# The low part of every second v block, subtracted by GpSimd instead of VectorE

## The chip, the cores and the metric

The kernel runs on one core of a Trainium2 chip. The metric is the device time of one execution in microseconds; lower is better. The median of three runs of the kernel before is 2388.8 us (2382.14 to 2390.61).

## The reference

One inference step of a two-layer encoder trunk for two groups of requests: 256 prompt rows and 8 x 16 sample rows, each row 1024 wide. Layer 0 mixes rows by a short gated convolution, layer 1 by stick-breaking attention; after each comes PEER, a mixture of 16384 single-row experts per layer, of which every row chooses 8 x 16 by product keys:

```python
def block(xb):
    q = (xb @ w_q).reshape(PEER_BLOCK, PEER_HEADS, 2, PEER_HALF).astype(jnp.float32)
    s = jnp.einsum("thpc,hpnc->thpn", q, subkeys.astype(jnp.float32))
    s_top, i_top = lax.top_k(s, K)
    ...
    g = jax.nn.softmax(best, axis=-1)
    act = jax.nn.gelu(jnp.einsum("td,thkd->thk", xb, u_tab[expert]), approximate=False)
    wgt = (g * act.astype(jnp.float32)).astype(xb.dtype)
    return jnp.einsum("thk,thkd->td", wgt, v_tab[expert])
```

Each mixer and each PEER is followed by x <- LayerNorm(ALPHA * x + sublayer(x)).

## The kernel before, in words

The two groups take different ways. The **sample rows** gather their experts: `peer_gather` fetches, for each of the 128 chosen experts of a row, the rows of u and of v by indirect DMA from GpSimd's queue (`gather`, L354) into one of four `row` buffers; VectorE takes the dot product with u (L367), and adds the weighted v to the result (L372). That is 256 gathers and 256 VectorE steps per layer.

The **prompt rows** go through all experts of a layer (`peer_dense`), 128 blocks of 128 experts, two blocks (a pair) at a time, with gates that are zero where an expert is not chosen. Of each pair, `a_pair` computes the first product u h and its gelu (TensorE into a `pg` bank, L147 to L149; ScalarE L393 into `lag`); two blocks later in the order, VectorE multiplies with the gates G (`wt`, L457), and the second product w v is summed into four `acc` banks over all blocks. The first product runs four blocks (AHEAD) in front of the second. 14 of the 64 first products are made before the gates are there.

Float32 operands are **split** into a high and a low part, and three matmuls stand for one (`mm3`): ScalarE copies to the high part (L107, `whi`, `uhi`, `vhi`), and VectorE subtracts it from the source for the low part (L108, `wlo`, `ulo`, `vlo`). For a pair that is two u blocks and two v blocks of 128x1024, and one w of 128x512, all inputs in SBUF. `split_v` takes its results from a pool of two buffers (`vhl`), so that each block of a pair has one; the source blocks are loaded by SP's queue into `wv` (three buffers, first block of the pair) and `more` (two buffers, second block).

The sample rows' gathers run beside the passes over the experts: those of layer 0 beside the first pass (about 480 to 1118 us) and the prompt's normalization behind it, those of layer 1 beside the second pass (about 1728 to 2362 us).

The order of the instructions on each engine is fixed when the program is built: a planner simulates the work with its own costs and lists each engine's instructions in the order in which they come out ready. On the chip each engine takes its list strictly in order and waits for semaphores. GpSimd's list holds in the passes nothing but indirect gathers, VectorE's the splits, the gates and the gathers' steps.

Of the kernel before, what the change touches and what calls it, by code (L numbers as in the profile page):

```python
# [7 lines left out]
F32 = mybir.dt.float32  # L8
# [13 lines left out]
T = 384  # L22
TP = 256
ALPHA = 4.0 ** 0.25
NEG = -1.0e30
CAND = [(0, 1, 16), (1, 1, 8), (2, 1, 5), (3, 1, 4), (4, 1, 3), (5, 3, 2), (8, 8, 1)]
NCAND = 50
# those of them with (a + 1)(b + 1) <= 8, as (a's start and count, b's count): only they can be among the best 8
# [4 lines left out]
EARLY = 14  # pairs of blocks whose first product precedes the gates  # L33
KEEP = 4  # of them in SBUF until they are used, the others in DRAM
AHEAD = 4  # blocks by which the first product runs ahead of the second
# [3 lines left out]
def trunk(ctx: ExitStack, tc: tile.TileContext, I, O):  # L39
# [31 lines left out]
    with ExitStack() as es:  # L71
        tmp = pool("ctmp", right=True, scope=es)
        jp = tmp.tile([P, P], F32, name="jp")
        blk = tmp.tile([P, P], F32, name="blk")
        scr = tmp.tile([P, P], F32, name="scr")
        same = tmp.tile([P, P], F32, name="same")
        pblk = tmp.tile([P, 1], F32, name="pblk")
        kw = dict(channel_multiplier=0, allow_small_or_imprecise_dtypes=True)
        nc.gpsimd.iota(jp, pattern=[[1, P]], base=0, channel_multiplier=-1, allow_small_or_imprecise_dtypes=True)
        nc.gpsimd.iota(blk.rearrange("p (a b) -> p a b", b=16), pattern=[[1, 8], [0, 16]], base=0, **kw)  # L80
        nc.gpsimd.iota(places, pattern=[[1, NCAND], [0, 8]], base=0, **kw)
        start = [0]
        for a0, na, nb in CAND:
            start += [start[-1] + nb * (i + 1) for i in range(na)]
        o = 0
        for a0, na, nb in CAND8:
            for i in range(a0, a0 + na):
                nc.gpsimd.tensor_copy(places8[:, o:o + nb, :], places[:, start[i]:start[i] + nb, :])
                o += nb
        nc.vector.tensor_scalar(ident, jp, 0.0, None, op0=OP.is_equal)  # L90
        # trig[k', k] = 1 where k' >= k
        nc.vector.tensor_scalar(trig, jp, 0.0, None, op0=OP.is_le)
        nc.vector.memset(ones, 1.0)
        # same[p, j] = 1 where p and j lie in the same block of 16
        nc.vector.scalar_tensor_tensor(scr, ident, 1.0, blk, op0=OP.mult, op1=OP.mult, accum_out=pblk)
        nc.vector.tensor_scalar(same, blk, pblk, None, op0=OP.is_equal)
        nc.vector.tensor_mul(trib, trig, same)
        # maskb[k, q]: 0 where k < q and both lie in the same block, else NEG or less
        nc.vector.tensor_scalar(maskb, same, 1.0, -NEG, op0=OP.subtract, op1=OP.mult)
        nc.vector.scalar_tensor_tensor(maskb, trig, NEG, maskb, op0=OP.mult, op1=OP.add)  # L100
        nc.vector.memset(eps, 1e-5)
        nc.sync.dma_start(wdw, I["wdw"])

# [1 line left out]
    def split(hi, lo, src):  # L105
        """src = hi + lo exactly, each of float32r's 12 significant bits"""
        nc.scalar.activation(hi, src, AF.Copy)  # L107
        return nc.vector.tensor_sub(lo, src, hi.bitcast(F32))  # L108
# [7 lines left out]
    def in_turn(this, that):  # L116
        """this behind that on their engine, which so changes its tables of functions less often"""
        tc.add_manual_dep(this.ins, that.ins.name, mybir.DependencyInfo(
            mybir.DependencyClass.NoSync, mybir.DependencyReason.SCHED_ONLY), reason="fewer loads of tables")
# [19 lines left out]
    def split_v(w):  # L139
        hi = vhl.tile([P, D], F32R, name="vhi")  # L140
        lo = vhl.tile([P, D], F32R, name="vlo")
        split(hi, lo, w)
        return hi, lo

    def mm3(pt, L, R, first, last):
        """pt (+)= L^T R for operands in two parts"""
        nc.tensor.matmul(pt, lhsT=L[0], rhs=R[0], start=first, stop=False)  # L147
        nc.tensor.matmul(pt, lhsT=L[0], rhs=R[1], start=False, stop=False)  # L148
        nc.tensor.matmul(pt, lhsT=L[1], rhs=R[0], start=False, stop=last)  # L149

    def proj3(pt, w, hT, n):
        """pt[:, :n] = w^T hT, w: parts of 8 chunks of 128x128, hT: parts [128, 8, n]"""
        for c in range(NB):
            cs = slice(c * P, (c + 1) * P)
            mm3(pt[:, :n], [x[:, cs] for x in w], [x[:, c, 0:n] for x in hT], c == 0, c == NB - 1)

    def proj1(pt, w, hT):
        """pt = w^T hT in float32"""
# [34 lines left out]
    def transposed(r, dsts, ps):  # L193
        """write r^T into each of dsts (parts (hi, lo) [128, 8, 128], or one float32 tile)"""
# [15 lines left out]
    def topk_half(chains, small):  # L210
        """the 16 best of s [128, 128] and their places, in order; step by step for all chains (tv, ti, n, s)"""
# [12 lines left out]
    def stage2(tv, ti, al, g, e, nh=8):  # L224
        """experts e [128, 8, 16] (float32) and softmax gates g [128, 8, 16] of the 16 best pairs of each head.
        Only the pairs (a, b) with (a + 1)(b + 1) <= 16 can be among them: the others have 16 before them.
        tv: the best keys' values, and room behind them for as many numbers of keys"""
        # kind and head in one dimension: sums of values, then numbers of experts
# [29 lines left out]
        for k0, x, pl in ((0, ex8, places8), (8, ex, places)):  # L258
# [3 lines left out]
            # the numbers once for each rank, side by side  # L262
# [12 lines left out]
        # the sums of the cells: ever again the first half onto the second, in front of an odd one out  # L275
# [18 lines left out]
    def softmax(g, sm):  # L294
        """of each head's values less their maximum"""
# [5 lines left out]
    def from_pool(pl):  # L301
        """shapes count words of 4 bytes"""
        return lambda name, shape, dt=F32: pl.tile([P] + shape[:-1] + [shape[-1] * 4 // mybir.dt.size(dt)], dt, name=name)

    def from_arena(ar, start=0):
        """places in ar one after the other"""
# [13 lines left out]
    def route_prompt(tv, ti, al, xj, xd, gT, t):  # L320
        """of the 128 experts of tile t's tokens: the first keys x and the second keys y, as rows x, y and y^2 in two
        parts of 7 bits of every token, 4 tokens to a group and 16 groups to a block of 32 rows, into xj; the gates,
        into gT [128 k, 256 t]"""
# [27 lines left out]
    def gather(tab, ei, k):  # L351
        """rows of tab for the k-th experts of all tokens"""
# [26 lines left out]
    def peer_dense(L, hT, dn):  # L379
        """-> psum banks [2 tiles * 2 halves] of the sum over the experts"""  # L380
        lag, kept, early = {}, {}, {}

        def a_pair(i, pl, ps, native=False):
            """gelu(u h) of two blocks, with or without splitting u"""
# [11 lines left out]
        # some pairs while VectorE is busy with the routing  # L396
# [16 lines left out]
        # gates G[j, group, t, i] of the experts (group * 16 + i, j); the last four groups wait in DRAM  # L413
        G = dn.gp.tile([P, 4, TP, GI], F32, name="G")
        Gd = dram.tile([P, 4, TP, GI], F32, name="Gd")
        for t0 in range(0, TP, 4):
            us = slice(t0, t0 + 4)
            # i - x and (j - y)^2 of all places in a row and column, for 4 tokens
# [25 lines left out]
        for s in range(-AHEAD, NBLK, 2):  # L444
# [17 lines left out]
            vs = [split_v(load_v(I["pvn"][L, s + k], (wv, more)[k])) for k in range(2)]  # L462
            # the last two blocks by tiles, so that the first tile's normalization starts early
# [7 lines left out]
    def finish(pts, L_ln, hd, last, hT, hTf=None):  # L471
        """residual and layernorm of the two prompt tiles"""
        # the table of square roots, before the data is there
# [30 lines left out]
    def half_out(xT, name, n):  # L504
        """columns n * 512.. of x @ w, in psum"""
# [8 lines left out]
    def attn_sample(h):  # L514
        with ExitStack() as es:
# [8 lines left out]
            # block-diagonal queries [2 x 64 dims, (b, head, q)], and the mask in that order of columns  # L524
# [18 lines left out]
            # two pairs of heads at a time; columns of a pair: keys of the cache, new keys  # L543
# [53 lines left out]
    def route_sample_alone(h, L, then=None):  # L597
        """-> the experts' rows in the tables, by chunks of two heads, and the gates"""
# [32 lines left out]
    def attn_prompt(hT):  # L631
        """-> o-projection in psum banks; the scope's pools stay until es closes"""
        with ExitStack() as es:
# [19 lines left out]
            # columns of one head: keys 0..127 x all queries (256) | keys 128..255 x queries 128..255  # L653
# [48 lines left out]
    def best_keys(hT, hTf, L, dests, native=()):  # L702
        """per (head, half): scores of all tiles' tokens and their 16 best; dests: (tv, ti) per tile;
        native: the n with undivided operands"""
# [23 lines left out]
    class Dense:  # L728
        """the pools of a layer's pass over the experts, in the order in which they close"""
# [14 lines left out]
    def ranked(at):  # L744
        """what is traced here comes, where engines are contended, at the place of the mark"""
# [96 lines left out]
def _layout(i):  # L842
# [10 lines left out]
    def cols(w, n):  # [1024, n*128] -> [n][128 p][8 c * 128]  # L853
# [17 lines left out]
    # constants: by rows (x, y, two parts of y^2 of each of 4 tokens, 1, 1) the terms of i - x and of (j - y)^2  # L871
# [38 lines left out]
```

## Time and profile of the kernel before

| | us |
|---|---|
| median of the runs | 2388.8 |
| span of the profiled execution | 2374.8 |
| TensorE busy | 2271.8 (96%) |
| VectorE busy | 1918.5 (81%) |
| ScalarE busy | 1050.3 (44%) |
| GpSimd busy | 800.2 (34%) |
| DMA queues, share of 16 engines' span: SP's 45.3%, GpSimd's gathers and loads | 38.5% |
| mean granted TensorE clock | 0.978 |

PE is TensorE (PEld its weight loads), DVE VectorE, ACT ScalarE, POOL GpSimd. How the rows below are read:

- A row of busy times by stage gives the stretch in us from the span's start, its length, the busy us and instruction count (x) of PE, PEld, DVE, ACT and POOL, the granted TensorE clock as a share of full speed, the busy share of the DMA engines, and GB/s.
- A row of waits names the engine and step that waited, after "<-" what ended the wait, then the us in total, the times, and the longest.
- A row of instruction groups gives line, engine, operation, output <- inputs, shape and count, then busy us and the mean ns of one, then the engine's idle us just before them and what ended most of it.
- A row of a timeline gives start us, duration us, engine, line, operation, output <- inputs, shape and count, and in brackets the engine's idle time before it. Durations include a few hundredths of a microsecond that overlap with the next instruction.

### The profile page before, as it was taken

The page shows a single profiled execution, that of the slowest core. Times are in us where ns is not written, and L with a number is a line of the kernel's source. Part 1 is how long each engine was busy: PE and PEld are TensorE (multiplying, and loading weights), DVE is VectorE, ACT ScalarE, POOL GpSimd, SP SyncE. Part 2 cuts the span into 40 slices and gives each one's busy share as a digit, 9 for nine tenths or more (in the row PEclk, how much of TensorE's full clock was granted, in tenths as well). Part 3 has the DMA queues.
Part 4 walks back from the last instruction along what each step waited for, and adds up shares of the span by engine and source line. Part 5 has one row for each costly group of instructions (what it writes and reads, how often), then busy time and mean ns, then how long its engine had stood idle before and what let it go on. Part 6 is the DMA issues. An engine that isn't in the chain of part 4 may idle for free.

```text
span 2374.8 us, 37270 instructions
## 1 busy us (share of the span) xinstructions
PE 2271.8 (96%) x13708; PEld 1981.6 (83%) x13708; DVE 1918.5 (81%) x3493; ACT 1050.3 (44%) x1579; POOL 800.2 (34%) x659
## 2 busy tenths in 40 slices
PE   8979989999999999998799888988999999999997
PEld 8969876688888889887589677876698888888986
DVE  6559997898888889888623489987898888888888
ACT  3333325744444444443346432135644444444443
POOL 0002342353332343444221223443453332344442
PEclk9989998999999999999899999998999999999999
DMA  4556898999999999998976558989999999999996
GB/s 163 195 193 212 291 339 265 299 369 347 346 325 327 341 330 323 335 335 289 332 243 206 162 194 298 337 287 292 294 373 342 347 329 325 341 320 329 335 326 220
DMA packets 225928, 704.13 MB, mean 297 GB/s; under 512 B 24912, under 2 KB 59472, under 8 KB 224720
## 3 DMA queue, kind: packets, MB, share of 16 engines
q1 hardware_dynamic: 137200, 382.93, 45.3%
q0 software_dynamic: 87968, 318.28, 38.5%
q8 instruction: 108, 1.77, 0.3%
q14 instruction: 76, 0.62, 0.1%
q10 hardware_dynamic: 576, 0.52, 0.1%
HBM read 671.17 MB, written 30.48 MB: 295 GB/s over the span
## 4 chain that ended last, share of the span: by engine, by line
PE 80%; DVE 12%; DMA 5%; issue 2%; ACT 1%; POOL 0%; SPq 0%; DVEq 0%; ACTq 0%; POOLq 0%
PE acc L148 13%; PE acc L149 13%; PE acc L147 13%; PE pg L147 8%; PE pg L149 8%; PE pg L148 8%; PE pg L430 6%; PE ms L160 3%; PE acc L422 3%; DVE row L367 2%; DMA row<-in_pu,ei 2%; DMA row<-in_pv,ei 1%; PE ms L511 1%; DVE h L372 1%; DMA wv<-in_pvn 1%
## 5 line engine op out<-in xcount | busy, mean ns | idle before, releaser
L354 POOL DMA_INDIRECT row<-in_pv,ei x256 | 387.6, 1514 | 580.7 <-DVE h L372 448.4
L354 POOL DMA_INDIRECT row<-in_pu,ei x256 | 333.6, 1303 | 544.6 <-DVE row L367 409.4
L147 PE MATMUL pg<-hThi,uhi 128*128 128x256 f32 x1600 | 451.6, 282 | 0.0
L149 PE MATMUL pg<-hThi,ulo 128*128 128x256 f32 x1600 | 451.4, 282 | 0.0
L148 PE MATMUL pg<-hTlo,uhi 128*128 128x256 f32 x1600 | 451.3, 282 | 0.0
L108 DVE TENSOR_TENSOR vlo<-wv,vhi 128x1024 fp32r<-128x1024 f32 x280 | 341.9, 1222 | 89.4 <-ACT vhi L107 86.0
L107 ACT ACTIVATE vhi<-wv 128x1024 fp32r<-128x1024 f32 x280 | 295.3, 1055 | 259.9 <-PE acc L149 187.1
L148 PE MATMUL acc<-vlo,whi 128*128 128x512 f32 x1024 | 403.9, 394 | 0.1
L149 PE MATMUL acc<-vhi,wlo 128*128 128x512 f32 x1024 | 403.4, 395 | 0.0
L108 DVE TENSOR_TENSOR ulo<-wu,uhi 128x1024 fp32r<-128x1024 f32 x264 | 322.0, 1220 | 100.7 <-ACT uhi L107 91.0
L107 ACT ACTIVATE uhi<-wu 128x1024 fp32r<-128x1024 f32 x264 | 278.9, 1056 | 261.2 <-issue 92.5
L147 PE MATMUL acc<-vhi,whi 128*128 128x512 f32 x1024 | 345.5, 394 | 0.6 <-ACT whi L107 0.6
L372 DVE SCALAR_TENSOR_TENSOR h<-row,wg,h 128x1024 f32<-128x1024 f32 x256 | 327.4, 1279 | 18.7 <-DMA row<-in_pv,ei 18.3
L367 DVE SCALAR_TENSOR_TENSOR row<-row,h 128x1024 f32<-128x1024 f32 x256 | 310.5, 1216 | 13.8 <-DMA row<-in_pu,ei 13.7
L147 PEld LDWEIGHTS pg<-hThi,uhi 128*128 128x128 f32 x1600 | 304.7, 190 | 10.3
L148 PEld LDWEIGHTS pg<-hTlo,uhi 128*128 128x128 f32 x1600 | 304.7, 190 | 8.4
L149 PEld LDWEIGHTS pg<-hThi,ulo 128*128 128x128 f32 x1600 | 304.9, 191 | 5.3
L160 PE MATMUL acc<-arena,wu 128*128 128x256 f32 x1024 | 233.7, 387 | 17.3 <-DMA wu<-in_put 12.3
L160 PEld LDWEIGHTS acc<-arena,wu 128*128 128x128 f32 x1024 | 195.6, 194 | 49.7 <-DMA wu<-in_put 15.8
L149 PEld LDWEIGHTS acc<-vhi,wlo 128*128 128x128 f32 x1024 | 192.5, 188 | 40.3
L148 PEld LDWEIGHTS acc<-vlo,whi 128*128 128x128 f32 x1024 | 193.0, 188 | 37.5 <-DVE vlo L108 0.6
L147 PEld LDWEIGHTS acc<-vhi,whi 128*128 128x128 f32 x1024 | 187.8, 189 | 34.7 <-ACT whi L107 0.8
(261 smaller groups left out, 3244.7 us busy)
## 6 DMA issues: line engine op xcount, KB each, us to landing
wv<-in_pvn SPq DMA_DIRECT2D x256, 512.0 KB, 5.9
wu<-in_put SPq DMA_DIRECT2D x256, 512.0 KB, 6.2
row<-in_wpq POOLq DMA_DIRECT2D x32, 512.0 KB, 4.9
wu<-in_wpq SPq DMA_DIRECT2D x32, 512.0 KB, 5.2
Gd<-st SPq DMA_DIRECT2D x64, 256.0 KB, 5.4
G<-Gd SPq DMA_DIRECT2D x8, 2048.0 KB, 10.6
wu<-in_win SPq DMA_DIRECT2D x24, 512.0 KB, 3.5
early<-lag SPq DMA_DIRECT2D x20, 256.0 KB, 5.8
```

Source lines behind the costliest of these rows:

```text
L107: nc.scalar.activation(hi, src, AF.Copy)
L108: return nc.vector.tensor_sub(lo, src, hi.bitcast(F32))
L147: nc.tensor.matmul(pt, lhsT=L[0], rhs=R[0], start=first, stop=False)
L148: nc.tensor.matmul(pt, lhsT=L[0], rhs=R[1], start=False, stop=False)
L149: nc.tensor.matmul(pt, lhsT=L[1], rhs=R[0], start=False, stop=last)
L160: nc.tensor.matmul(pt, lhsT=w[:, c * P:(c + 1) * P], rhs=hT[:, c, :], start=(c == 0), stop=(c == NB - 1))
L354: nc.gpsimd.indirect_dma_start(out=row, out_offset=None, in_=tab, in_offset=bass.IndirectOffsetOnAxis(ap=ei[k // 32][:, k % 32:k % 32 + 1] ...
L367: nc.vector.scalar_tensor_tensor(u, u, 1.0, h, op0=OP.mult, op1=OP.mult, accum_out=dot[:, k:k + 1])
L372: nc.vector.scalar_tensor_tensor(r, v, wg[:, k:k + 1], r, op0=OP.mult, op1=OP.add)
L422: nc.tensor.matmul(pt, lhsT=xj[q:q + 18, t0 % 64 // 4, :], rhs=near[q:q + 18, k, :], start=True, stop=True)
L430: nc.tensor.matmul(pt[:, t * P:(t + 1) * P], lhsT=oj[:, t, :], rhs=oi[:, t, :], start=True, stop=True)
L511: nc.tensor.matmul(pt, lhsT=xT[:, c + i, :], rhs=w[:, i, :], start=(c + i == 0), stop=(c + i == 7))
```

## The change

In the passes over the experts, the second v block of every pair gets its low part from GpSimd's `tensor_sub` instead of VectorE's. `split` and `split_v` take the engine as an argument; all other splits stay with VectorE, and the high part stays with ScalarE. The same source lines without comments are otherwise the same program; line numbers stay.

```diff
-    def split(hi, lo, src):
-        """src = hi + lo exactly, each of float32r's 12 significant bits"""
+    def split(hi, lo, src, eng=nc.vector):
+
         nc.scalar.activation(hi, src, AF.Copy)
-        return nc.vector.tensor_sub(lo, src, hi.bitcast(F32))
+        return eng.tensor_sub(lo, src, hi.bitcast(F32))
...
-    def split_v(w):
+    def split_v(w, eng=nc.vector):
         hi = vhl.tile([P, D], F32R, name="vhi")
         lo = vhl.tile([P, D], F32R, name="vlo")
-        split(hi, lo, w)
+        split(hi, lo, w, eng)
         return hi, lo
...
-            vs = [split_v(load_v(I["pvn"][L, s + k], (wv, more)[k])) for k in range(2)]
+            vs = [split_v(load_v(I["pvn"][L, s + k], (wv, more)[k]), (nc.vector, nc.gpsimd)[k]) for k in range(2)]
```

## Rows read from the trace of the kernel before

**Rows 1.** Busy times by stage: the two passes, and behind the mixers.

```profile
480.00:1112.00 632.00, 631.26 (x3859) 564.25 (x3858) 550.69 (x590) 295.51 (x343) 239.26 (x157) 1.00 0.92 336
1112.00:1150.00 38.00, 21.81 (x84) 16.57 (x83) 35.58 (x47) 9.27 (x12) 16.97 (x13) 0.73 0.82 275
...
1404.00:1430.00 26.00, 19.03 (x123) 16.99 (x122) 24.52 (x101) 9.67 (x21) 9.62 (x12) 0.87 0.78 271
...
1728.00:2360.00 632.00, 632.00 (x3854) 564.71 (x3853) 552.07 (x578) 293.65 (x340) 246.12 (x153) 1.00 0.92 331
```

**Rows 2.** TensorE's waits: the only one in 480 to 1112, and one of all.

```profile
PE acc L147 <- ACT whi L107: 0.6, 1, 0.6
...
PE pg L198 <- DVE wu L186: 23.2, 3, 14.3
```

**Rows 3.** Groups of VectorE's instructions in 480 to 1112, by shape.

```profile
L108 DVE TENSOR_TENSOR vlo<-wv,vhi 128x1024 fp32r<-128x1024 f32 x126 | 153.9, 1221 | 25.2 <-ACT vhi L107 23.0 <-DMA wu<-in_put 1.3
...
L372 DVE SCALAR_TENSOR_TENSOR h<-row,wg,h 128x1024 f32<-128x1024 f32 x79 | 101.1, 1279 | 0.1
```

**Rows 4.** VectorE's four largest waits in 480 to 1112.

```profile
DVE vlo L108 <- ACT vhi L107: 23.0, 35, 2.2
DVE ulo L108 <- ACT uhi L107: 20.4, 24, 2.9
DVE wt L457 <- ACT lag L393: 15.3, 12, 3.0
DVE wlo L108 <- ACT whi L107: 11.7, 20, 1.3
```

**Rows 5.** GpSimd's two largest waits in 480 to 1112.

```profile
POOL row L354 <- DVE h L372: 193.3, 74, 10.0
POOL row L354 <- DVE row L367: 188.7, 77, 6.6
```

**Rows 6.** Timelines of ScalarE, VectorE, TensorE, GpSimd: one second block of a pair.

```profile
808.27 1.05 ACT L107 ACTIVATE vhi<-wv 128x1024 fp32r<-128x1024 f32 x1
...
809.40 1.23 DVE L108 TENSOR_TENSOR vlo<-wv,vhi 128x1024 fp32r<-128x1024 f32 x1
...
814.14 0.40 PE L148 MATMUL acc<-vlo,whi 128*128 128x512 f32 x1
...
808.61 1.71 POOL L354 DMA_INDIRECT row<-in_pv,ei  x1 [5.70 <-DVE h L372]
```

**Rows 7.** Groups of GpSimd's instructions, by shape: two of its copies.

```profile
L88 POOL COPY places<-places 128x8 bf16<-128x8 bf16 x4 | 0.8, 348 | 0.0
...
L88 POOL COPY places<-places 128x64 bf16<-128x64 bf16 x1 | 0.4, 397 | 0.0
```

**Rows 8.** Timelines of VectorE and GpSimd in the first 5 us.

```profile
1.85 2.22 DVE L96 TENSOR_SCALAR same<-blk,pblk 128x128 f32<-128x128 f32 x1
4.10 0.32 DVE L97 TENSOR_TENSOR trib<-trig,same 128x128 f32<-128x128 f32 x1
4.34 0.21 DVE L99 TENSOR_SCALAR maskb<-same 128x128 f32<-128x128 f32 x1
...
2.00 1.90 POOL L407 MEMSET xj<- 128x2048 bf16 x1
```

**Rows 9.** Timelines of TensorE and VectorE behind the first pass.

```profile
1132.69 1.94 PE L198 MATMUL pg<-ident,wu 128*128 128x128 f32 x8 [14.33 <-DVE wu L186]
...
1164.89 2.60 DVE L372 SCALAR_TENSOR_TENSOR h<-row,wg,h 128x1024 f32<-128x1024 f32 x2
```

**Rows 10.** VectorE's timeline at the end: last steps of samples and prompt.

```profile
2358.66 1.41 DVE L186 SCALAR_TENSOR_TENSOR h<-h,rs,gb 128x512 f32<-128x512 f32 x2
...
2368.15 2.74 DVE L186 SCALAR_TENSOR_TENSOR wu<-wu,rs,gb 128x512 f32<-128x512 f32 x4
```

## The prediction

> **What bounds the kernel now.** I read first the busy times by stage. In both passes over the experts (480 to 1112 us and 1728 to 2360 us) TensorE is busy 631.3 and 632.0 of 632.0 us at a granted clock of 1.00, VectorE 550.7 and 552.1, GpSimd 239.3 and 246.1 [rows 1]. So in these stretches TensorE sets the pace. The list of TensorE's waits agrees: one wait of 0.6 us in the whole first pass [rows 2]. Taking work off VectorE can't make a stretch shorter in which TensorE never waits for VectorE. Outside the passes TensorE does idle: 16.2 of 38 us where the first pass ends (1112 to 1150), 7.0 of 26 us at 1404 [rows 1].
>
> Next I read what fills VectorE in the first pass: among others 126 low parts of v of 1221 ns, and 79 second-half gather steps (L372) of 1279 ns for the sample rows [rows 3]. These gathers run beside the passes and end just behind the first (last one at 1164.89, [rows 9]) and just before the end of the second. VectorE idles 632.0 - 550.7 = 81.3 us in the pass; four waits for ScalarE make 23.0 + 20.4 + 15.3 + 11.7 = 70.4 us of it [rows 4].
>
> **Removed.** 64 subtractions of a pass leave VectorE, 64 x 1.221 = 78.1 us per pass [rows 3]. TensorE gains nothing by that directly [rows 2].
>
> **Added on GpSimd.** 64 subtractions of 128x1024 in float32 with two inputs. No row shows GpSimd doing this. Nearest are its copies: 348 ns for 8 elements and 397 ns for 64 [rows 7], so (397 - 348) / 56 = 0.875 ns per element and 341 ns fixed. If both inputs stream together: 341 + 0.9 us = 1.24 us. If the two reads follow each other: 341 + 1.79 us = 2.13 us. If the write too takes its turn: 3.03 us. I take 2.13, the middle one, since a subtraction has one read more than the copy. That is 136 us per pass, and GpSimd's busy time goes to 239.3 + 136.3 = 375.6 of 632 us, so it has room. By the page GPSIMD Engine Reference of the Trainium skill (section Performance versus the Vector engine), an add of 2048 float32 takes 4497 ns there, half of which is an estimate of 2.25 us; no run here shows it yet, and with it the sum below would be about 15 us higher.
>
> **The new wait.** The step now stands in GpSimd's queue among the gathers. What is queued behind it: the next indirect gathers; who waits for those: L367 and L372 on VectorE, and behind them in VectorE's order ulo, wt and wlo. What stands before it: a gather that waits for a row buffer, 193.3 us in 74 waits and 188.7 us in 77 (2.5 us each, longest 10.0) [rows 5]. The cover: in a typical pair, the one at 808 us, ScalarE ends vhi of the second block at 808.27 + 1.05 = 809.32, VectorE starts vlo at 809.40, and the first matmul that reads it starts at 814.14 [rows 6]; I take this pair for the pattern of the 64. So a subtraction has 4.8 us where it needs 2.1, plus what it waits for a gather ahead of it (1.71 us for the one at 808.61 [rows 6]). Costed at nothing as long as this sum stays under 4.8 us; each microsecond over that is one of TensorE's. SP's queue keeps its loads and their order; a v block that is read later holds its buffer (of two) a microsecond or two longer, against 632 / 64 = 9.9 us per pair.
>
> **The shared way into SBUF.** This is the term that decides. The trace has one collision of the two engines: at 1.85 us VectorE's L96 took 2.22 us, while GpSimd's memset of xj ran from 2.00 for 1.90 us; the like operation L99, of the same size, took 0.21 [rows 8]. So a VectorE instruction can stand still through a whole GpSimd instruction. Against it: L97 (two inputs from SBUF) took 0.32 us for 128 columns beside GpSimd's small copies, which is hardly stretched [rows 8], and all subtractions beside gathers average 1221 ns [rows 3]. Copies of 8 to 64 elements and gathers hardly read SBUF, so they are further from the case than L96. Bounds of what VectorE loses per moved subtraction: nothing, and the whole 2.13 us (3.03 with the longest price). I take the whole, by L96. The Trainium skill's page SBUF — State Buffer (section Who interferes with whom) says that a VectorE instruction with two SBUF inputs contends with a GpSimd instruction that reads SBUF, and that the one that starts second is blocked to the first one's end. Every elementwise step of the pass on VectorE is of that kind. By that rule L97 would have been held up too had the copies beside it been long; no run here shows such a pair yet.
>
> Then VectorE has 550.7 - 78.1 + 136.3 = 608.9 us of work and blocking in 632 us. Of its 81.3 us idle I take half, 40.7, as time that it can't use, because it waits for ScalarE, which itself waits for TensorE; ends: none of it and all of it. 608.9 + 40.7 = 649.6, so 17.6 us per pass don't fit and show as waits of TensorE or as a longer gather tail: 35.2 us for two passes (with all idle usable 0, with none 58.2 per pass, 116).
>
> **The tail of the first pass.** Sixteen of TensorE's idle microseconds there are a normalization whose steps alternate on VectorE with the last gathers (TensorE waits 14.3 us at 1132.69 [rows 9]). If the planner fills the freed slots with gathers, some of this comes back: at best the 10 us by which this wait exceeds an undisturbed one (estimate from the two other waits of that kind, 23.2 - 14.3 us for both [rows 2]), at worst nothing. I take 5. At the end the samples' last step ends at 2358.66 + 1.41 = 2360.07 and the prompt's at 2368.15 + 2.74 = 2370.89 [rows 10]: a later gather has 10.8 us before it costs.
>
> **Sum.** The profiled span is 2374.8 us; the median of the runs is 14.0 us above it, taken as time outside the span. 2374.8 + 35.2 - 5 + 14.0 = 2419.
>
> **Rivals.**
> A, faster: no blocking. The two engines work side by side, VectorE has 78 us more per pass, the gathers of the first pass end before it does, and the normalization behind it and the v products run undisturbed. For it: the 1221 ns beside gathers, L97; against: L96. Price: 10 us from the wait at 1132.69, and some 5 us from the rest of 1112 to 1200: 2374. It decides as long as VectorE's rows in the pass stay near 1.22 us.
> B, no change: VectorE is blocked, but its idle time takes it all (all 81.3 us usable, 608.9 of 632), and GpSimd's step stays within its 4.8 us. For it: the 70 us of waits for ScalarE vanish where VectorE comes late. 2389.
> C, much slower: the subtraction itself gets no turn, since VectorE's instructions stand back to back, or it stands behind a gather that waits for a late VectorE. Once the delay passes 4.8 us TensorE waits. Price: a step of 2.13 us behind one of the longer gather waits (4 us) is 1.3 us late; in half of the pairs of both passes 64 x 1.3 = 83 us, over B's time: 2472.
> That the change doesn't move what it says is no rival of weight: the engine is fixed by the line, and only the planner's order around it is open; that case falls under B.
>
> **How the numbers follow.** Chances: forecast 0.45, A 0.22, B 0.20, C 0.13. A measurement of this kernel can tell about 0.5% (12 us) from no change. Faster by more: most of A, and a little of the forecast with the tail's full gain, 0.20. Within: B, the rest of A and the low end of the forecast, 0.27. Slower: the rest of the forecast and C, 0.53. The range leaves out 1 in 10 at each side: from A's time less its spread, 2371, to C's, 2475; the forecast's own range is 2395 to 2450.
>
> **What would show it.** In the passes: VectorE's L108, L367 and L372 stretched from 1.22 to means of 1.5 us and more, with single ones over 3 us, shows the blocking (if not, A). A GpSimd row vlo x128 of near 2.1 us, or far over it, sizes the step. TensorE waits "acc L148 <- POOL vlo" show lateness of the step (C); waits for ulo, wlo or whi show VectorE's backlog (the forecast). The last L372 of the first pass before 1115 shows the tail's gain, after 1170 a loss. The prediction is wrong if TensorE's 631 of 632 us stays as it is and the stage 1112 to 1200 gets shorter.

## The result and the profile after

The kernel after takes 2411.4 us in the median of four runs (2404.86 to 2413.52), the kernel before 2385.8 us beside it (2382.14 to 2390.61): a ratio of 1.0108, with an interval of 1.0074 to 1.0142. So it is slower, by 25.7 us. The profiled execution of after took 2404.86 us, its span 2403.1 us; what lies around a span is 1.8 us.

First the busy times by stage of after; columns as in [rows 1].

```profile
480.00:1112.00 632.00, 628.29 (x3833) 561.02 (x3832) 577.72 (x522) 292.21 (x340) 420.48 (x217) 1.00 0.91 333
1112.00:1150.00 38.00, 21.22 (x88) 15.44 (x86) 36.85 (x45) 10.60 (x14) 21.31 (x14) 0.82 0.80 259
1173.00:1393.00 220.00, 211.86 (x1368) 181.53 (x1368) 75.84 (x144) 103.65 (x168) 40.65 (x72) 0.91 0.58 194
1728.00:2360.00 632.00, 626.35 (x3857) 558.50 (x3856) 588.04 (x511) 293.73 (x354) 410.21 (x217) 1.00 0.91 330
```

In the passes VectorE lost 64 subtractions and is yet busier: 577.7 us against 550.7 in the first, 588.0 against 552.1 in the second [rows 1]. TensorE, which waited once in the first pass, for 0.6 us [rows 2], is now busy 628.3 and 626.4 us. The third line is a stage that the change doesn't touch, attention; its granted clock is 0.91. The same stretch of before:

```profile
1173.00:1393.00 220.00, 213.94 (x1490) 185.13 (x1489) 88.45 (x220) 109.06 (x179) 44.13 (x78) 0.99 0.63 207
```

In the same 220 us, the last 20 of which lie behind attention in before, before gets 1490 matmuls done, after 1368, at a busy share that hardly differs. So two places got longer, and the next table has them for all kernels of this study, by the timelines of TensorE. A pass runs from its first matmul of the second product (acc<-vhi,whi) to its last; attention from the last high-part matmul of the prompt's projection to v (acc<-vhi,hThi) to the first of its output projection (acc<-vhi,oThi); keys and gates from the last of that projection to the first second product of layer 1. Short stretches between these are left out. In brackets are the us of a stage at the lower of the two levels of the granted clock (0.5, 1.2 GHz; the rest ran at 2.4 GHz). One profiled execution each.

| kernel | span | to the first second product | pass 1 | attention | keys and gates of layer 1 | pass 2 |
|---|---|---|---|---|---|---|
| before | 2374.8 | 483.3 (38) | 634.6 | 205.0 (3) | 323.9 (27) | 634.1 |
| before_again | 2380.7 | 487.5 (48) | 634.5 | 209.6 (17) | 321.4 (27) | 634.1 |
| after | 2403.1 | 481.4 (34) | 641.8 (3) | 221.6 (41) | 324.1 (20) | 641.9 |
| l1_only | 2390.0 | 489.0 (55) | 634.5 | 210.2 (17) | 320.5 (24) | 643.0 (7) |
| l0_to112_l1 | 2390.1 | 485.7 (44) | 639.5 | 210.2 (14) | 320.7 (27) | 640.2 |
| l0_last8 | 2395.2 | 491.2 (51) | 635.5 | 218.4 (34) | 323.6 (24) | 634.0 |
| no_low_part | 2411.7 | 486.1 (44) | 634.7 | 221.3 (48) | 340.8 (44) | 634.6 |
| write_only | 2397.9 | 482.7 (38) | 634.7 | 214.7 (38) | 337.0 (38) | 634.6 |
| copy_one_input | 2391.2 | 483.7 (38) | 635.1 | 221.9 (41) | 322.0 (17) | 634.1 |
| both_blocks | 2488.5 | 480.8 (38) | 699.9 (20) | 211.3 (17) | 320.4 (31) | 688.8 (17) |

Between the profiles of before and after the passes account for 7.2 + 7.8 = 15.0 us and attention for 16.6; the other stages give back some 3. The profiled execution of before lies below its median: 2374.8 + 1.8 = 2376.6 us against 2385.8.

What happened in the passes is seen in the groups of VectorE's instructions of after from 480 to 1112 us, and in GpSimd's group of the whole span (columns as in [rows 3]).

```profile
L108 DVE TENSOR_TENSOR ulo<-wu,uhi 128x1024 fp32r<-128x1024 f32 x98 | 157.3, 1610 | 25.9 <-ACT uhi L107 25.7
L372 DVE SCALAR_TENSOR_TENSOR h<-row,wg,h 128x1024 f32<-128x1024 f32 x78 | 125.9, 1614 | 0.6 <-DMA row<-in_pv,ei 0.5
L367 DVE SCALAR_TENSOR_TENSOR row<-row,h 128x1024 f32<-128x1024 f32 x77 | 110.9, 1446 | 0.2 <-DMA row<-in_pu,ei 0.2
L108 DVE TENSOR_TENSOR vlo<-wv,vhi 128x1024 fp32r<-128x1024 f32 x62 | 75.6, 1219 | 11.7 <-ACT vhi L107 11.6
```

```profile
L108 POOL TENSOR_TENSOR vlo<-wv,vhi 128x1024 fp32r<-128x1024 f32 x128 | 359.2, 2806 | 80.1 <-ACT vhi L107 78.3
```

L372, 1279 ns before [rows 3], now takes 1614 in the mean, and ulo 1610; ulo in the same stretch of before:

```profile
L108 DVE TENSOR_TENSOR ulo<-wu,uhi 128x1024 fp32r<-128x1024 f32 x98 | 119.6, 1220 | 26.5 <-ACT uhi L107 20.4 <-ACT vhi L107 5.1 <-issue 0.5
```

The 62 steps left of vlo, the first blocks', are not stretched (1219). The stretch is not even; single instructions take it whole. Two timelines of after, first VectorE's, then GpSimd's:

```profile
599.38 0.68 DVE L108 TENSOR_TENSOR wlo<-wt,whi 128x512 fp32r<-128x512 f32 x1
599.98 3.81 DVE L372 SCALAR_TENSOR_TENSOR h<-row,wg,h 128x1024 f32<-128x1024 f32 x1
603.71 1.21 DVE L108 TENSOR_TENSOR ulo<-wu,uhi 128x1024 fp32r<-128x1024 f32 x1
```

```profile
600.29 2.41 POOL L108 TENSOR_TENSOR vlo<-wv,vhi 128x1024 fp32r<-128x1024 f32 x1
```

L372 takes 3.81 us where it needs 1.28: longer by 2.53, about the 2.41 of the subtraction beside it. TensorE's waits in after, in the stretch of the first pass and of the second (columns as in [rows 2]):

```profile
PE acc L148 <- POOL vlo L108: 3.2, 3, 2.4
PE acc L148 <- DVE vlo L108: 1.3, 2, 1.2
```

```profile
PE acc L148 <- POOL vlo L108: 6.1, 6, 2.3
```

They are few, but they are most of what the passes lost: 4.5 us in the first, which got 7.2 us longer, and 6.1 in the second, which got 7.8. No other wait of TensorE is listed there; of the rest, the 3 us at the lower clock cost some 1.5 in the first pass. What held TensorE up were low parts from GpSimd that came late, and in the first pass, for 1.3 us, two from VectorE. Why GpSimd's came late is seen at the longest wait of the first pass, in timelines of GpSimd, VectorE and TensorE:

```profile
537.72 5.82 POOL L108 TENSOR_TENSOR vlo<-wv,vhi 128x1024 fp32r<-128x1024 f32 x1
```

```profile
536.80 1.28 DVE L372 SCALAR_TENSOR_TENSOR h<-row,wg,h 128x1024 f32<-128x1024 f32 x1
538.00 2.36 DVE L108 TENSOR_TENSOR ulo<-wu,uhi 128x1024 fp32r<-128x1024 f32 x2
540.27 1.07 DVE L457 TENSOR_TENSOR wt<-lag,G 128x512 f32<-128x512 f32 x1
541.25 3.38 DVE L372 SCALAR_TENSOR_TENSOR h<-row,wg,h 128x1024 f32<-128x1024 f32 x1
```

```profile
543.60 0.80 PE L148 MATMUL acc<-vlo,whi 128*128 128x512 f32 x1 [2.37 <-POOL vlo L108]
```

Four steps of VectorE that follow each other directly (L372, two ulo, wt) keep their usual length, while the subtraction takes 3.4 us longer than the 2.4 it needs; only the next L372 is stretched, and TensorE waits 2.37 us. Two more waits, of 2.33 and 1.16 us, end on subtractions that took 5.83 and 4.73 us; two, of 1.50 and 0.46, on subtractions of usual length that began behind two gathers.

### The profile page after: what moved, and what is told of

It reads as the page before. It is cut to its first block, busy times and chain, and to the rows that moved or that the text cites. A ratio compares the mean times of both kernels' runs of the same rounds, so it can differ in the third digit from the quotient of the medians.

```text
span 2403.1 us, 37300 instructions
## 1 busy us (share of the span) xinstructions
PE 2289.8 (95%) x13708; PEld 1992.3 (83%) x13708; DVE 1996.0 (83%) x3365; ACT 1048.2 (44%) x1579; POOL 1154.0 (48%) x787
## 4 chain that ended last, share of the span: by engine, by line
PE 64%; DVE 13%; issue 9%; POOL 7%; DMA 6%; ACT 1%; SPq 0%; POOLq 0%; DVEq 0%; ACTq 0%
PE acc L149 11%; PE acc L148 11%; PE acc L147 11%; PE pg L147 6%; PE pg L149 6%; PE pg L148 6%; POOL row L354 5%; PE pg L430 3%; PE ms L160 3%; DVE row L367 2%; POOL vlo L108 2%; PE acc L422 2%; DMA row<-in_pu,ei 1%; DMA row<-in_pv,ei 1%; PE ms L511 1%
## 5 line engine op out<-in xcount | busy, mean ns | idle before, releaser
L354 POOL DMA_INDIRECT row<-in_pv,ei x256 | 369.9, 1445 | 355.8 <-DVE h L372 233.2
L354 POOL DMA_INDIRECT row<-in_pu,ei x256 | 346.1, 1352 | 366.8 <-DVE row L367 245.1
L108 DVE TENSOR_TENSOR ulo<-wu,uhi 128x1024 fp32r<-128x1024 f32 x264 | 394.8, 1500 | 92.9 <-ACT uhi L107 86.7
L147 PE MATMUL pg<-hThi,uhi 128*128 128x256 f32 x1600 | 451.2, 282 | 0.0
L149 PE MATMUL pg<-hThi,ulo 128*128 128x256 f32 x1600 | 451.2, 282 | 0.0
L372 DVE SCALAR_TENSOR_TENSOR h<-row,wg,h 128x1024 f32<-128x1024 f32 x256 | 393.5, 1537 | 20.1 <-DMA row<-in_pv,ei 19.5
L149 PE MATMUL acc<-vhi,wlo 128*128 128x512 f32 x1024 | 404.5, 396 | 0.0
L108 POOL TENSOR_TENSOR vlo<-wv,vhi 128x1024 fp32r<-128x1024 f32 x128 | 359.2, 2806 | 80.1 <-ACT vhi L107 78.3
L367 DVE SCALAR_TENSOR_TENSOR row<-row,h 128x1024 f32<-128x1024 f32 x256 | 348.3, 1366 | 9.0 <-DMA row<-in_pu,ei 8.7
L147 PE MATMUL acc<-vhi,whi 128*128 128x512 f32 x1024 | 336.5, 394 | 0.0
L147 PEld LDWEIGHTS pg<-hThi,uhi 128*128 128x128 f32 x1600 | 304.4, 190 | 10.6
L149 PEld LDWEIGHTS pg<-hThi,ulo 128*128 128x128 f32 x1600 | 304.6, 190 | 6.3
L108 DVE TENSOR_TENSOR vlo<-wv,vhi 128x1024 fp32r<-128x1024 f32 x152 | 188.4, 1239 | 56.4 <-ACT vhi L107 56.2
L149 PEld LDWEIGHTS acc<-vhi,wlo 128*128 128x128 f32 x1024 | 193.0, 189 | 39.3
```

The source lines that it names most:

```text
L108: return eng.tensor_sub(lo, src, hi.bitcast(F32))
L354: nc.gpsimd.indirect_dma_start(out=row, out_offset=None, in_=tab, in_offset=bass.IndirectOffsetOnAxis(ap=ei[k // 32][:, k % 32:k % 32 + 1] ...
L367: nc.vector.scalar_tensor_tensor(u, u, 1.0, h, op0=OP.mult, op1=OP.mult, accum_out=dot[:, k:k + 1])
L372: nc.vector.scalar_tensor_tensor(r, v, wg[:, k:k + 1], r, op0=OP.mult, op1=OP.add)
```

## The experiments

Two questions were open. First, do two engines that read SBUF block each other, or is the time of the passes something else? Second, what made attention longer? Two theories for the second: the blocking reaches it somehow through the late gathers, or the planner, which prices the moved step otherwise, lists the instructions of attention in another order. All kernels below have the changed `split` and `split_v` of after unless told otherwise; the diffs are against after.

### One layer only

```diff
-            vs = [split_v(load_v(I["pvn"][L, s + k], (wv, more)[k]), (nc.vector, nc.gpsimd)[k]) for k in range(2)]
+            vs = [split_v(load_v(I["pvn"][L, s + k], (wv, more)[k]), nc.gpsimd if k and L == 1 else nc.vector) for k in range(2)]
```

> Only the second pass (layer 1) has the subtraction on GpSimd; the order of all engines up to that pass is that of the kernel before. If the loss is blocking of VectorE inside a pass plus an order of the attention stage that the first pass's change brought about, then the stages up to 1728 us stay as before, the second pass grows by 8 us and the total by 8 us (about 2394). If the moved subtraction costs the same 14 us per layer wherever it goes, the total grows by 13 to 14 us (2399).

Measured: 2395.3 us (2391.81 to 2403.13) against 2380.7, a ratio of 1.0064 (1.0046 to 1.0082), 14.6 us slower. In the table pass 2 is 643.0, 8.9 us longer, and pass 1 as before, so each pass pays for its own subtractions. The total is no answer to the second question: it is 5.7 us over what the pass shows. Against before_again the profile is 9.3 us longer, 8.9 of them the pass. Against before it is 15.2 us longer, and stages that stand ahead of every moved step, and whose matmuls stand in the very order of before, have 10.9 of that: 5.7 up to the first second product (489.0 us, 55 of them at the low clock, against 483.3 (38), and 487.5 (48) in before_again) and 5.2 in attention. So the clock moves the time of a stage with one and the same order by some 5 us between executions (over all ten kernels, whose order is the same up to the first second product, by 10: 480.8 to 491.2), and smaller differences of a stage tell nothing in a single profile. The surplus of the medians goes with the clock too: the granted clock of a whole execution is 0.969 to 0.975 here and 0.973 to 0.977 in the eleven of before. Whether chance alone makes it stays open.

### All but the last eight moved subtractions of layer 0

```diff
-            vs = [split_v(load_v(I["pvn"][L, s + k], (wv, more)[k]), (nc.vector, nc.gpsimd)[k]) for k in range(2)]
+            vs = [split_v(load_v(I["pvn"][L, s + k], (wv, more)[k]), nc.gpsimd if k and (L == 1 or s < 112) else nc.vector) for k in range(2)]
```

> GpSimd subtracts in layer 0 for the first 56 of 64 pairs and in all of layer 1; TensorE's order in the attention stage is then that of the kernel before. Order theory: both passes grow by 7 to 8 us, the stretch between them stays at 610 us, total 14 to 15 us over before (2400). Rival, the time between the passes grows because gathers of layer 0 end late through the blocking: 120 of 128 moved subtractions are left, so it grows by 13 to 15 us again and the total by 26 to 28 us (2413).

Measured: 2394.6 us (2391.85 to 2413.2), 1.0076 (1.0048 to 1.0103), 13.9 us slower. With 120 of 128 subtractions moved, the passes take 639.5 and 640.2 (+4.9 and +6.1), and attention, whose matmuls stand in the order of before here, 210.2 (14), as in before_again. That is less than the 7 to 8 expected, though in the second pass all 64 are moved; still, most of the passes' loss is here, and attention isn't touched by it.

### The last eight alone

```diff
-            vs = [split_v(load_v(I["pvn"][L, s + k], (wv, more)[k]), (nc.vector, nc.gpsimd)[k]) for k in range(2)]
+            vs = [split_v(load_v(I["pvn"][L, s + k], (wv, more)[k]), nc.gpsimd if k and L == 0 and s >= 112 else nc.vector) for k in range(2)]
```

> Only the last 8 pairs of layer 0 have the subtraction on GpSimd, 8 in the whole kernel; TensorE's order in the attention stage is that of the changed kernel. Order theory: passes as before within 1 us, the stretch between them 625 us with several stretches of granted clock 0.5 in 1200 to 1400, total 13 to 17 us over before (2400). Rival, blocking: 8 of 128 moved subtractions, so under 2 us (2387).

Measured: 2396.4 us (2389.38 to 2409.34), 1.0072 (1.0045 to 1.0098), 15.7 us slower. Eight moved subtractions cost in the median as much as 120, and elsewhere: the passes are 635.5 and 634.0, attention is 218.4 with 34 us at the low clock, 8.8 longer than in before_again. (Another 3.7 against before_again lie ahead of the first pass, where the order is the same: the scatter of the clock.) Attention's matmuls stand in the order of after. That settles the second question for the order. What the order does is seen in TensorE's timeline of l0_last8, where its clock falls (at 1280.5 us):

```profile
1274.61 1.87 PE L586 MATMUL ms<-z,row 128*128 128x32 f32 x16
1276.40 0.70 PE L667 MATMUL pg<-qkp 64*128 64x256 f32 x2
1277.03 1.97 PE L553 MATMUL ms<-qd,row 128*128 128x32 f32 x16
1278.84 0.68 PE L555 MATMUL ms<-qd,kn 128*128 128x256 f32 x2
1279.45 0.48 PE L668 MATMUL pg<-qkp 64*128 64x128 f32 x2
1279.86 3.03 PE L553 MATMUL ms<-qd,row 128*128 128x32 f32 x16
```

and of before_again at the like place:

```profile
1269.55 1.95 PE L553 MATMUL ms<-qd,row 128*128 128x32 f32 x16
1271.34 0.68 PE L555 MATMUL ms<-qd,kn 128*128 128x256 f32 x2
1271.67 0.47 PE L147 MATMUL acc<-hThi,uhi 128*128 128x256 f32 x1
1271.97 0.28 PE L148 MATMUL acc<-hTlo,uhi 128*128 128x256 f32 x1
...
1272.80 1.87 PE L553 MATMUL ms<-qd,row 128*128 128x32 f32 x16
```

The samples' matmuls of 32 columns (L586, L553) come in sixteens. In before's order eight dense matmuls (L147 to L149) stand between the two sixteens of L553, in after's they stand elsewhere, and the second sixteen takes 3.03 us instead of 1.87. TensorE isn't idle before the clock falls; the busy times by stage of l0_last8 just before, around and after it show it busy throughout, and the clock going from 1.00 to 0.50:

```profile
1270.00:1279.00 9.00, 9.00 (x72) 8.47 (x71) 1.92 (x2) 3.56 (x8) 1.06 (x2) 1.00 0.69 224
1279.00:1282.00 3.00, 3.00 (x18) 2.55 (x18) 1.28 (x4) 1.26 (x2) 0.53 (x1) 0.76 0.71 220
1282.00:1290.00 8.00, 8.00 (x32) 6.94 (x32) 2.76 (x6) 5.13 (x7) 0.53 (x1) 0.50 0.25 89
```

In after and copy_one_input, which have this order too, it falls at 1277.4 and 1275.9 us, at the same place in the order, and an earlier fall of l0_last8 at 1249.8 us has its like in them at 1246.7 and 1245.2. With before's order (before, before_again, l1_only, l0_to112_l1) attention has 3, 17, 17 and 14 us at the low clock, at changing places; with after's (after, l0_last8, copy_one_input) 41, 34 and 41. About half of the low time is what the clock costs: in before, matmuls of 128x512 that follow each other directly (L147 to L149) start 0.43 us apart at 1140 us, at the lower level, and 0.23 apart at 1144, at the higher. Attention less this half is 203.5, 201.1, 201.7 and 203.2 with the one order, 201.1, 201.4 and 201.4 with the other. So the clock is the difference, to within some 2 us. What in the order decides the clock was not tried by itself: that it is the sixteens that stand together is read from these timelines, not shown by a kernel that moves nothing else.

### The kernel before once more

This is the kernel before, unchanged: no edit.

> The kernel before, profiled a second time. Order theory: the stretch of the prompt's and the samples' attention takes 205 to 211 us with at most 20 us at the lower clock level, as in the runs that share its order, against 218 to 222 us with 34 to 48 us in the runs with another order. If instead the clock falls there by chance, it may as well show 218 us or more; then the 16 us between the passes of the changed kernel are noise of single profiles.

Measured: 2382.5 us, with attention at 209.6 (17). So 4 to 5 of the 16.6 us in attention are the first profile's low value of 205.0, not the change.

### No low part for the second block

The low part of the second v block is left out, and its high part stands in for it, so TensorE has the same matmuls.

```diff
+        if eng is None:
+            nc.scalar.activation(hi, w, AF.Copy)
+            return hi, hi
         lo = vhl.tile([P, D], F32R, name="vlo")
...
-            vs = [split_v(load_v(I["pvn"][L, s + k], (wv, more)[k]), (nc.vector, nc.gpsimd)[k]) for k in range(2)]
+            vs = [split_v(load_v(I["pvn"][L, s + k], (wv, more)[k]), None if k else nc.vector) for k in range(2)]
```

> The low part of the second v block isn't computed at all; its high part stands in for it in the matmuls, so that TensorE's work is the same and the results are not the reference's. VectorE is relieved of 78 us per pass with nothing added to GpSimd. If TensorE bounds the passes, both stay at 632 to 634 us, the relief shows as idle time of VectorE or as earlier gathers, and the total lies within 15 us of before (2371 to 2390), less only by what the stretch between the passes gains or loses through the order. If VectorE held the passes up in a way the waits don't show, they get shorter by more than 5 us each.

Measured: 2413.4 us (2402.75 to 2414.59), 1.0121 (1.0095 to 1.0146), 32.7 us slower than before, with less work. VectorE is down to 481 us in the first pass, and the passes stay:

```profile
480.00:1112.00 632.00, 632.00 (x3877) 566.14 (x3876) 481.34 (x530) 296.45 (x343) 215.84 (x157) 1.00 0.93 336
1728.00:2360.00 632.00, 632.00 (x3889) 561.35 (x3889) 483.47 (x532) 301.31 (x376) 214.47 (x161) 1.00 0.93 335
```

634.7 and 634.6 us: relief of VectorE is worth nothing there. That the total would stay near before was wrong. The planner made yet another order: attention has 221.3 us (48 low), and keys and gates 340.8 (44 low). The clock explains (44 - 27) / 2 = 8.5 of the 16.9 us by which keys and gates are longer. In this order 54 of the matmuls that before does within attention stand behind it, which may be part of the rest; it was not followed up.

### GpSimd that only writes

The low part of the second block is left out; GpSimd writes two memsets of its size instead.

```diff
-        return eng.tensor_sub(lo, src, hi.bitcast(F32))
+        return [nc.gpsimd.memset(lo.bitcast(F32), 0.0) for _ in range(2)] if eng == "write" else eng.tensor_sub(lo, src, hi.bitcast(F32))
...
-            vs = [split_v(load_v(I["pvn"][L, s + k], (wv, more)[k]), (nc.vector, nc.gpsimd)[k]) for k in range(2)]
+            vs = [split_v(load_v(I["pvn"][L, s + k], (wv, more)[k]), "write" if k else nc.vector) for k in range(2)]
```

> In place of the subtraction GpSimd fills the low part of the second v block with zeros by two memsets: as many engine microseconds in the same queue, roughly 2 us, but no read of SBUF; the low part is left out of the result. If VectorE's two-input instructions are blocked by GpSimd's reads alone, ulo, L367 and L372 stay at 1.22 to 1.28 us and both passes at 634 to 636 us. If any GpSimd instruction of that length blocks them, their means go to 1.4 to 1.5 us and the passes to 640 us.

Measured: 2399.7 us against 2388.4 on the same chip, with passes of 634.7 and 634.6. The rows of GpSimd's memsets (durations in ns: least, median, greatest) and of L372's group over the whole span:

```profile
L108 POOL MEMSET vlo<- x256: 951/957/1008, 164.5 to 2377.8; 128x1024 f32 x128
```

```profile
L372 DVE SCALAR_TENSOR_TENSOR h<-row,wg,h 128x1024 f32<-128x1024 f32 x256 | 327.2, 1278 | 16.2 <-DMA row<-in_pv,ei 15.5
```

Neither engine is stretched, though GpSimd works 1.9 us for every pair here; the 86 L372 that overlap with a memset have a mean of 1280 ns. (The memsets wait for no high part, so this kernel doesn't show what GpSimd's queue alone would make late.) What the kernel loses, it loses in attention and in keys and gates, as no_low_part does, whose order of matmuls it has in both.

### GpSimd that reads one input

GpSimd copies the block instead of subtracting; the low part is thus not the reference's.

```diff
-        return eng.tensor_sub(lo, src, hi.bitcast(F32))
+        return nc.gpsimd.tensor_copy(lo, src) if eng == "copy" else eng.tensor_sub(lo, src, hi.bitcast(F32))
...
-            vs = [split_v(load_v(I["pvn"][L, s + k], (wv, more)[k]), (nc.vector, nc.gpsimd)[k]) for k in range(2)]
+            vs = [split_v(load_v(I["pvn"][L, s + k], (wv, more)[k]), "copy" if k else nc.vector) for k in range(2)]
```

> In place of the subtraction GpSimd copies the v block into the low part: one read of SBUF and one write, and the low part is not the reference's. If reading SBUF blocks VectorE for the whole instruction, single VectorE steps of the passes are stretched by the copy's own length (estimate 1.2 us from the fixed 341 ns and 0.875 ns per element), the mean of ulo goes to 1.3 to 1.4 us, and the passes grow by 1 to 4 us. If only two-input GpSimd work blocks, the steps stay at 1.22 us and the passes at 634 to 635 us.

Measured: 2393.0 us. GpSimd's copies and two groups of VectorE:

```profile
L108 POOL CAST vlo<-wv x128: 1041/1240/2823, 487.2 to 2372.6; 128x1024 fp32r<-128x1024 f32 x128
```

```profile
L372 DVE SCALAR_TENSOR_TENSOR h<-row,wg,h 128x1024 f32<-128x1024 f32 x256 | 341.0, 1332 | 19.0 <-DMA row<-in_pv,ei 18.2
L108 DVE TENSOR_TENSOR wlo<-wt,whi 128x512 fp32r<-128x512 f32 x128 | 149.7, 1170 | 26.6 <-ACT whi L107 23.5 <-PE pg L149 2.9
```

The same group of before:

```profile
L108 DVE TENSOR_TENSOR wlo<-wt,whi 128x512 fp32r<-128x512 f32 x128 | 88.2, 689 | 30.0 <-ACT whi L107 28.4 <-PE pg L148 0.8 <-PE pg L149 0.6
```

Now both are stretched: wlo to a mean of 1170 ns from 689, the copies from 1.04 us to as much as 2.82. So a GpSimd step that reads one input is enough, and one that only writes isn't. Of the expectation, the stretch came on wlo and hardly on ulo (1245 ns), and the passes didn't grow (635.1 and 634.1): VectorE is busy 523.9 us in the first, 26.8 less than before, since a copy of 1.04 us costs it less than the 1.22 that it was rid of.

### Both blocks

```diff
-            vs = [split_v(load_v(I["pvn"][L, s + k], (wv, more)[k]), (nc.vector, nc.gpsimd)[k]) for k in range(2)]
+            vs = [split_v(load_v(I["pvn"][L, s + k], (wv, more)[k]), nc.gpsimd) for k in range(2)]
```

> GpSimd subtracts for both v blocks of a pair, 128 per pass. By blocking, VectorE has 550.7 - 156 + 128 x 2.42 x 0.86 (the share of the time in which it has work) = 661 us of work and blocking in a pass, more than TensorE's 632: both passes become 660 to 700 us long, with TensorE waiting for low parts, and the total grows by 60 to 140 us. If the cost of a moved subtraction were the 7.5 us per 64 seen so far, doubling gives 15 us per pass and 30 us in all beside what the order of the other stages does.

Measured: 2490.3 us, 102 us slower, with passes of 699.9 and 688.8. First pass and the groups of the whole span, of VectorE and of GpSimd; then TensorE's largest wait of the span:

```profile
480.00:1112.00 632.00, 596.34 (x3555) 524.87 (x3554) 609.05 (x432) 268.80 (x314) 529.45 (x257) 0.99 0.87 308
```

```profile
L372 DVE SCALAR_TENSOR_TENSOR h<-row,wg,h 128x1024 f32<-128x1024 f32 x256 | 471.6, 1842 | 24.4 <-DMA row<-in_pv,ei 22.7
```

```profile
L108 POOL TENSOR_TENSOR vlo<-wv,vhi 128x1024 fp32r<-128x1024 f32 x256 | 672.3, 2632 | 24.6 <-ACT vhi L107 20.6
```

```profile
PE acc L148 <- POOL vlo L108: 71.6, 68, 4.7
```

Twice the moved steps cost the passes 65 and 55 us instead of 7.2 and 7.8, as expected: VectorE has little idle time left (609 of 632 us busy), and GpSimd's steps are late for TensorE 68 times, by 71.6 us in all, where after has 9 times and 9.3 us. VectorE's backlog, by which the expectation got there, shows in 11 us of waits for its ulo and vlo. This is the prediction's rival C in full; after has the beginning of it.

## Why the prediction came out as it did

**What bounds the passes: right.** TensorE, with VectorE's relief worth nothing: no_low_part frees 69 us of VectorE in a pass, and the pass doesn't move.

**The shared way into SBUF: right in kind.** The decision for blocking, by the memset beside L96 [rows 8], held: 3.81 us beside 2.41. But L96 was an unlike row. It stood beside a memset, and write_only shows that memsets don't hold up the steps of the pass at all; the decision was right, the row didn't bear it. What bears it stood beside: by the Trainium skill's page SBUF — State Buffer (section Who interferes with whom) a VectorE step with two SBUF inputs contends with a GpSimd instruction that reads SBUF and not with one that only writes it. write_only, copy_one_input and after agree with each half of that. That the one that starts second is blocked to the first one's end holds only in part by the records: the subtraction at 537.72 us stood through four VectorE steps, three of which began behind it.

**The price of the subtraction: too low.** 2.13 us was taken; without a VectorE step in its way it takes 2.40 (least 2397 ns), inside the bounds of 1.24 to 3.03. The estimate of 2.25 us by the Trainium skill's page GPSIMD Engine Reference (section Performance versus the Vector engine) was nearer. Whether the two reads follow each other the runs don't tell: the copy with one read takes 1.04 us and the memset without one 0.96.

**The blocking term: 17.6 us per pass, measured 1.3 and nothing.** The sum had VectorE's work, its blocking and half of its idle time overflow the pass, and named waits of TensorE for ulo, wlo or whi as the sign of that. There are none; the only waits for VectorE are the 1.3 us for vlo in the first pass, and the gathers' tail, the other sign, is no longer than it was (see below). The passes did grow, by 7.2 and 7.8 us, but by the new wait, below. The parts of the term were off as well. The sum let every subtraction block VectorE for its whole length, 136.3 us in a pass. Estimated from the busy times of the stretches: 577.7 - (550.7 - 78.1) = 105.1 us in the first pass, and 588.0 - (552.1 - 78.1) = 114.0 in the second, 22 to 31 less than reckoned. That is 1.6 to 1.8 us per subtraction of 2.4, so about 0.7 of its time finds VectorE in want of the way. Against it, the idle time that VectorE can't use was taken as half, 40.7 us; its waits for ScalarE are still 52.9 us in the first pass of after (70.4 before, [rows 4]), 12 more than reckoned:

```profile
DVE ulo L108 <- ACT uhi L107: 25.7, 26, 3.1
DVE vlo L108 <- ACT vhi L107: 11.6, 9, 3.0
DVE wt L457 <- ACT lag L393: 10.9, 7, 3.8
DVE wlo L108 <- ACT whi L107: 4.7, 7, 1.2
```

The two together are 10 to 19 us below the sum. That the passes too came out 10 us below it confirms nothing: busy and idle time of VectorE always add up to the stretch, and what TensorE waited for is another thing.

**The new wait: costed at nothing, and it is what the passes lost.** The step was late for TensorE 3 times in the first pass and 6 in the second, by 3.2 and 6.1 us; the prediction named this sign for rival C. Both mechanisms of C are there, VectorE's steps back to back and gathers ahead in the queue, at 9.3 us instead of its 83. The reason given for nothing was the cover of 4.8 us [rows 6], which is about twice the step. It was no generous pair: read the same way, from the end of vhi to the first matmul that reads the block, 63 pairs of before's first pass have a median of 6.0 us, and three of them less than 4.8. But the forecast let GpSimd block VectorE and not VectorE block GpSimd, by which a step took up to 5.83 us. GpSimd's waits for a row buffer did fall, to 89.9 and 77.5 us from 188.7 and 193.3 [rows 5].

**The tail of the first pass: no gain.** 5 us were taken off. The wait of 14.3 us [rows 9] became 13.8; the last gather step of layer 0 ends at 1172.2 us instead of 1167.5, about as much later as the pass itself (1123.6 instead of 1118.4). That the freed slots of VectorE were blocked would explain it; no run shows it by itself.

```profile
PE pg L198 <- DVE wu L186: 13.8, 1, 13.8
```

**The sum's last term: wrong in what it was called.** 14.0 us were added as time outside the span. That time is 1.8 us; the other 12.2 is the distance of the profiled execution from the median. As a step from one profile to the median it did its work all the same.

**The step that is missing.** The prediction names the planner's order once, as open around the moved step, and files it under no change. Nothing in it let the order of a stage change that the edit doesn't touch. Attention has 221.6, 218.4 and 221.9 us with after's order, a mean of 220.6, and 205.0, 209.6, 210.2 and 210.2 with before's, 208.8: 11.9 us. With the passes' 15.0 that makes 26.9, against 25.7 measured in the medians. So the forecast of 30.2 us over before came near the result by errors that cancel: 20.2 us too much in the passes, 5 too little at the tail, and 11.9 that it didn't know of. The direction was earned, since the blocking is real and the longest of TensorE's waits come of it; the size is luck.

No kernel of this study is faster than before.

## What to carry to other kernels

When an elementwise step is moved from VectorE to GpSimd and both read SBUF, price it twice. It takes up to its whole length from VectorE as well: here 1.22 us saved and 1.6 to 1.8 lost for each, so VectorE got busier by the move, and its idle time kept nearly all of that from TensorE. And the moved step itself may stand through several VectorE steps, 5.8 us instead of 2.4, and be late for whoever waits for it: that is what TensorE felt. Ask first whether the engine that bounds the stage ever waits for the one that is relieved; where it doesn't, there is nothing to win. And where a planner makes the order, compare the length and the granted clock of every stage, also far from the edit, before the edit's own mechanism is given the whole difference: mostly by the order of a far stage, eight moved steps cost here as much as 120.

## What the runs showed of the hardware

- The two engines hold each other up, GpSimd through as many as four VectorE steps in a row. Of after's 128 subtractions 84 took 3.0 us in the mean, up to 5.83, and the VectorE step that was running when they began took its usual time, 1.2 us in the mean. The other 44 took 2.4 to 2.5 us; in 31 of them a VectorE step was on that the records show begun earlier (by 0.3 us in the median), and in 20 of these 31 that step was held (3.1 to 4.2 us). So the record's order of starts doesn't tell who is held.
- GpSimd's subtraction of 128x1024 in float32 takes 2.40 us, a copy 1.04, a memset 0.96; VectorE's subtraction takes 1.22.
- Taking work away can make a kernel slower: no_low_part does less and takes 32.7 us more, at a granted clock of 0.5 for 48 us of attention and 44 us of keys and gates, against 3 to 17 and 24 to 27 us with before's order.
- With one and the same order the low clock covered 3 to 17 us of attention from one execution to the next, and, over all ten kernels, 34 to 55 us of the stages ahead of the first pass.
